# Row standard deviation: two adjacent rows per load, statistics split by columns between two engines, shrinking last pieces

## The chip, the cores and the metric

The kernel runs on one core of a Trainium2 chip. The time is the device time of one execution in microseconds (us), as the median of several executions. The profile is one such execution; its span leaves out about 1.8 us that the time includes (641.0 against 642.8 here). The experiments ran in four batches on four chips, and the kernel before took 642.6 us in the first comparison and about 645 us in these batches, so kernels are compared by their ratio to the kernel before on the same chip.

Five engines matter: DVE (VectorE), ACT (ScalarE), POOL (GpSimd), SP, which only issues loads and output writes here, and the 16 DMA engines, which carry all loads together.

## The reference

```python
x = np.random.randn(8192, 8192).astype(np.float32)
def reference(x):
    return np.std(x, axis=1)
```

268.4 MB are read once and 8192 numbers come out. Every row is held by one of 128 partitions; "a row" below means one row in each partition, 4 MiB in all.

## The kernel before

Partition p owns rows 64p to 64p+63, so in step i the kernel reads 128 runs of 32 KiB that lie 64 rows apart in the input. Five buffers of one row each are in turn. DVE sums a row, ACT sums its squares in two halves, and the variance follows from the two sums. The last row is loaded and summed in two halves.

```python
    xrows = x.rearrange("(p i) m -> i p m", p=P, i=I)      # I = 64, C = 8192, CS = 4096
    rows = [(i, [0, C]) for i in range(I - 1)] + [(I - 1, [0, CS, C])]    # shortened
    xpool = ctx.enter_context(tc.tile_pool(name="xtiles", bufs=5))
    # ... cut ...
    def do_row(i, cuts):
        xt = xpool.tile([P, C], FP32, name="xt")
        for ci in range(len(cuts) - 1):
            c0, c1 = cuts[ci], cuts[ci + 1]
            nc.sync.dma_start(out=xt[:, c0:c1], in_=xrows[i][:, c0:c1])
            nc.vector.reduce_sum(out=asum[:, i - base, ci:ci + 1], in_=xt[:, c0:c1], axis=mybir.AxisListType.X)
            # ... cut: nsub pieces of step columns ...
                nc.scalar.activation(out=dummy[:, 0:step], in_=xt[:, s0:s0 + step],
                    func=mybir.ActivationFunctionType.Square,
                    accum_out=asq[:, i - base, ci + si:ci + si + 1])
    # ... cut: the first 62 rows are combined on POOL, the last two on DVE, then Sqrt and two output writes
```

Of the kernel before, what the change touches and what calls it, by code (L numbers as in the profile page):

```python
# [1 line left out]

# [4 lines left out]

FP32 = mybir.dt.float32


@with_exitstack
def kernel(
    ctx: ExitStack,
    tc: tile.TileContext,
    x: bass.AP,
    out: bass.AP,
):
    nc = tc.nc
    P = nc.NUM_PARTITIONS  # L20
    R, C = x.shape
    I = R // P
    N = float(C)
    inv_n = 1.0 / N
    CS = C // 2

    xrows = x.rearrange("(p i) m -> i p m", p=P, i=I)
    out_pi = out.rearrange("(p i) -> p i", p=P)

    NB = I - 2  # L30
    rows = []
    for i in range(I - 1):
        rows.append((i, [0, C]))
    rows.append((I - 1, [0, CS, C]))

    xpool = ctx.enter_context(tc.tile_pool(name="xtiles", bufs=5))
    stats = ctx.enter_context(tc.tile_pool(name="stats", bufs=1))
    psum = ctx.enter_context(tc.tile_pool(name="psumdump", bufs=1, space=bass.MemoryType.PSUM))

    dummy = psum.tile([P, CS], FP32)  # L40

    NT = I - NB
    sumA = stats.tile([P, NB, 4], FP32)
    sqA = stats.tile([P, NB, 4], FP32)
    sumB = stats.tile([P, NT, 4], FP32)
    sqB = stats.tile([P, NT, 4], FP32)
    nc.vector.memset(sumB, 0.0)  # L47
    nc.vector.memset(sqB, 0.0)  # L48
    invn_t = stats.tile([P, 1], FP32)
    nc.vector.memset(invn_t, inv_n)  # L50

    def do_row(i, cuts):
        asum, asq, base = (sumA, sqA, 0) if i < NB else (sumB, sqB, NB)
        xt = xpool.tile([P, C], FP32, name="xt")
        for ci in range(len(cuts) - 1):
            c0, c1 = cuts[ci], cuts[ci + 1]
            nc.sync.dma_start(out=xt[:, c0:c1], in_=xrows[i][:, c0:c1])  # L57
            nc.vector.reduce_sum(  # L58
                out=asum[:, i - base, ci:ci + 1],
                in_=xt[:, c0:c1],  # L60
                axis=mybir.AxisListType.X,
            )
            nsub = (c1 - c0 + CS - 1) // CS
            step = (c1 - c0) // nsub
            for si in range(nsub):
                s0 = c0 + si * step
                nc.scalar.activation(  # L67
                    out=dummy[:, 0:step],
                    in_=xt[:, s0:s0 + step],
                    func=mybir.ActivationFunctionType.Square,  # L70
                    accum_out=asq[:, i - base, ci + si:ci + si + 1],
                )

    vA = stats.tile([P, NB], FP32)

    for (i, cuts) in rows:
        do_row(i, cuts)
        if i == NB - 1:
            tsqA = stats.tile([P, NB], FP32)
            nc.gpsimd.tensor_add(tsqA, sqA[:, :, 0], sqA[:, :, 1])  # L80
            t0 = stats.tile([P, NB], FP32)
            nc.gpsimd.tensor_mul(t0, sumA[:, :, 0], sumA[:, :, 0])  # L82
            nc.gpsimd.tensor_mul(t0, t0, invn_t.to_broadcast((P, NB)))  # L83
            nc.gpsimd.tensor_sub(vA, tsqA, t0)  # L84

    tsqB = stats.tile([P, NT], FP32)
    nc.vector.reduce_sum(out=tsqB, in_=sqB, axis=mybir.AxisListType.X)  # L87
    tsumB = stats.tile([P, NT], FP32)
    nc.vector.reduce_sum(out=tsumB, in_=sumB, axis=mybir.AxisListType.X)  # L89
    m2 = stats.tile([P, NT], FP32)  # L90
    nc.vector.scalar_tensor_tensor(  # L91
        out=m2, in0=tsumB, scalar=inv_n, in1=tsumB,
        op0=mybir.AluOpType.mult, op1=mybir.AluOpType.mult,
    )
    vB = stats.tile([P, NT], FP32)
    nc.vector.tensor_sub(vB, tsqB, m2)  # L96

    stdA = stats.tile([P, NB], FP32)
    nc.scalar.activation(out=stdA, in_=vA,  # L99
                         func=mybir.ActivationFunctionType.Sqrt, scale=inv_n)  # L100
    nc.sync.dma_start(out=out_pi[:, 0:NB], in_=stdA)
    stdB = stats.tile([P, NT], FP32)
    nc.scalar.activation(out=stdB, in_=vB,  # L103
                         func=mybir.ActivationFunctionType.Sqrt, scale=inv_n)
    nc.scalar.dma_start(out=out_pi[:, NB:I], in_=stdB)


# [1 line left out]
_INS = ['x']  # L109
_OUTS = [((8192,), 'float32')]  # L110


# [23 lines left out]
```

## Time and profile before

| what | value | where it stands |
|---|---|---|
| time | 642.79 us, 642.44 to 643.25 | three runs |
| DMA engines | 9 tenths or more in all but the first and last slices | page, busy tenths |
| a row lands every | 9.7 us, (39.8 + 8.7) / 5 | chain of waits |
| last input lands | 630.35 us | completion records |
| from there to the end | 10.7 us | 641.0 - 630.35 |

These are the last pieces of the chain of waits (start us, duration us, what):

```profile
571.74 8.70 DVE sumA L58
...
580.49 39.80 DMA xt<-in_x_dram
...
620.38 10.02 DVE sumB L58 x2
630.41 2.91 issue
633.31 4.41 DVE sumB L58
...
638.34 0.20 ACT stdB L103
```

Row 62 arrives at 620.3 us and row 63 at 630.35, but DVE needs 8.7 us a row and is busy until 637.7 (the 2.91 us that the chain calls issue are no idle time: DVE is at work on the first half of row 63). The stage table from 616 us on (stretch, length, busy time of DVE, ACT and POOL, clock, DMA share, GB/s) says the same:

```profile
616.00:620.00 4.00, 3.28 (x1) 3.39 (x3) 0.85 (x3) 1.00 0.90 385
620.00:624.00 4.00, 3.62 (x1) 3.54 (x2) 0.34 (x2) 1.00 1.00 426
624.00:628.00 4.00, 4.00 (x1) 3.97 (x4) 0.00 (x0) 1.00 0.97 410
628.00:632.00 4.00, 4.00 (x2) 3.94 (x4) 0.00 (x0) 1.00 0.14 51
632.00:636.00 4.00, 4.00 (x2) 3.54 (x2) 0.00 (x0) 1.00 0.00 0
636.00:640.00 4.00, 2.24 (x5) 0.20 (x1) 0.00 (x0) 1.00 0.02 0
```

### The profile page before, as it was taken

The numbers are of one execution on the slowest core, as the hardware profiler recorded it, in microseconds if no ns is written. First come the engines' busy times: TensorE is split into PE (matmuls) and PEld (weight loads), VectorE is DVE, ScalarE is ACT, GpSimd is POOL, SyncE is SP. The second block draws the span as 40 slices with busy tenths as digits, with TensorE's granted clock in tenths as the row PEclk, the third lists the DMA queues.
The fourth block names the chain that finished last, engine by engine and source line by source line (L and its number), as shares of the span: only waits on it lengthen the run. The fifth ranks groups of instructions, "written<-read, shape, count | busy, mean of one in ns | idle before, by whom it ended". The sixth has DMA issues, their size and how long they took to land.

```text
span 641.0 us, 576 instructions
## 1 busy us (share of the span) xinstructions
DVE 556.5 (87%) x72; ACT 477.9 (75%) x260; POOL 1.4 (0%) x8
## 2 busy tenths in 40 slices
DVE  1889889889889898898898898898898988988988
ACT  1767778778778778777787787787787787777886
POOL 0000000000000000000000000000000000000000
DMA  8999999999999999999999999999999999999992
GB/s 339 413 419 405 429 433 433 431 432 429 431 433 433 431 429 431 433 433 431 429 431 425 429 428 436 433 430 431 427 438 431 431 431 427 438 431 431 429 422 88
DMA packets 9653, 268.51 MB, mean 419 GB/s; under 512 B 1328, under 2 KB 1328, under 8 KB 1328
## 3 DMA queue, kind: packets, MB, share of 16 engines
q1 hardware_dynamic: 9504, 268.47, 97.9%
q14 instruction: 5, 0.04, 0.0%
q10 hardware_dynamic: 144, 0.00, 0.0%
HBM read 268.44 MB, written 0.03 MB: 419 GB/s over the span
## 4 chain that ended last, share of the span: by engine, by line
DMA 80%; DVE 19%; issue 1%; SPq 0%; ACT 0%; DVEq 0%
DMA xt<-in_x_dram 80%; DVE sumA L58 16%; DVE sumB L58 2%; SPq L57 0%; ACT stdB L103 0%; DVE vB L96 0%; DVE m L91 0%; DVE tsumB L89 0%; DVE tsqB L87 0%; DVEq L58 0%
## 5 line engine op out<-in xcount | busy, mean ns | idle before, releaser
L58 DVE TENSOR_REDUCE sumA<-xt 128x1 f32<-128x8192 f32 x62 | 538.5, 8686 | 79.8 <-DMA xt<-in_x_dram 79.8
L67 ACT ACTIVATE dummy<-xt 128x4096 f32<-128x4096 f32 x128 | 459.2, 3587 | 156.1 <-DMA xt<-in_x_dram 154.0
L67 ACT ACTIVATION_READ_ACCUMULATOR dummy<-xt 128x1 f32 x128 | 24.0, 187 | 0.0
L58 DVE TENSOR_REDUCE sumB<-xt 128x1 f32<-128x4096 f32 (+1 forms) x3 | 17.3, 5835 | 1.1 <-DMA xt<-in_x_dram 1.1
L103 ACT ACTIVATE stdB<-vB 128x2 f32<-128x2 f32 x1 | 0.2, 204 | 2.8 <-DVE vB L96 2.8
L67 ACT ACT_TABLE_LOAD x1 | 1.3, 1283 | 0.7 <-PEq L120 0.7
L80 POOL TENSOR_TENSOR tsqA<-sqA 128x62 f32<-128x62 f32 x1 | 0.3, 296 | 617.7 <-ACT dummy L67 617.7
L99 ACT ACT_TABLE_LOAD x1 | 1.3, 1283 | 0.0
L99 ACT ACTIVATE stdA<-vA 128x62 f32<-128x62 f32 x1 | 0.3, 257 | 1.0 <-POOL vA L84 1.0
L47 DVE MEMSET sumB<- 128x8 f32 x1 | 0.1, 65 | 0.8 <-PEq L120 0.8
L84 POOL TENSOR_TENSOR vA<-tsqA,t 128x62 f32<-128x62 f32 x1 | 0.3, 317 | 0.1
L82 POOL TENSOR_TENSOR t<-sumA 128x62 f32<-128x62 f32 x1 | 0.3, 295 | 0.9 <-DVE sumA L58 0.9
L83 POOL TENSOR_TENSOR t<-t,invn_t 128x62 f32<-128x62 f32 x1 | 0.3, 291 | 0.1
L96 DVE TENSOR_TENSOR vB<-tsqB,m 128x2 f32<-128x2 f32 x1 | 0.2, 161 | 0.0
L91 DVE SCALAR_TENSOR_TENSOR m<-tsumB 128x2 f32<-128x2 f32 x1 | 0.2, 160 | 0.0
L89 DVE TENSOR_REDUCE tsumB<-sumB 128x2 f32<-128x8 f32 x1 | 0.2, 161 | 0.0
L87 DVE TENSOR_REDUCE tsqB<-sqB 128x2 f32<-128x8 f32 x1 | 0.1, 149 | 0.0
L120 POOL MEMSET const-bfloat16-1.0<- 128x1 bf16 x1 | 0.1, 103 | 0.0
L120 POOL MEMSET const-uint8-127<- 128x1 uint8 x1 | 0.1, 103 | 0.0
L120 POOL MEMSET const-float32-0.0<- 128x1 f32 x1 | 0.1, 99 | 0.2 <-issue 0.2
L120 POOL MEMSET const-float32-1.0<- 128x1 f32 x1 | 0.1, 99 | 0.0
L48 DVE MEMSET sqB<- 128x8 f32 x1 | 0.1, 65 | 0.0
(1 smaller groups left out, 0.1 us busy)
## 6 DMA issues: line engine op xcount, KB each, us to landing
xt<-in_x_dram SPq DMA_DIRECT2D x63, 4096.0 KB, 39.8
xt<-in_x_dram SPq DMA_DIRECT2D x2, 2048.0 KB, 37.6
out_dram<-stdA SPq DMA_DIRECT2D x1, 31.0 KB, 9.8
out_dram<-stdB ACTq DMA_DIRECT2D x1, 1.0 KB, 1.4
```

What stands on the lines that cost most here:

```text
L58: nc.vector.reduce_sum(out=asum[:, i - base, ci:ci + 1], in_=xt[:, c0:c1], axis=mybir.AxisListType.X,)
L67: nc.scalar.activation(out=dummy[:, 0:step], in_=xt[:, s0:s0 + step], func=mybir.ActivationFunctionType.Square, accum_out=asq[:, i - base, ...
L80: nc.gpsimd.tensor_add(tsqA, sqA[:, :, 0], sqA[:, :, 1])
L82: nc.gpsimd.tensor_mul(t0, sumA[:, :, 0], sumA[:, :, 0])
L83: nc.gpsimd.tensor_mul(t0, t0, invn_t.to_broadcast((P, NB)))
L84: nc.gpsimd.tensor_sub(vA, tsqA, t0)
L89: nc.vector.reduce_sum(out=tsumB, in_=sumB, axis=mybir.AxisListType.X)
L91: nc.vector.scalar_tensor_tensor(out=m2, in0=tsumB, scalar=inv_n, in1=tsumB, op0=mybir.AluOpType.mult, op1=mybir.AluOpType.mult,)
L96: nc.vector.tensor_sub(vB, tsqB, m2)
L99: nc.scalar.activation(out=stdA, in_=vA, func=mybir.ActivationFunctionType.Sqrt, scale=inv_n)
L103: nc.scalar.activation(out=stdB, in_=vB, func=mybir.ActivationFunctionType.Sqrt, scale=inv_n)
L120: nc = _bacc.Bacc("TRN2", target_bir_lowering=False, num_devices=1)
```

## The change

The intent is a shorter end and fewer, larger loads. Each row is split by columns: DVE takes 5120 columns as ten statistics operations of 512 (mean and variance in one pass), ACT takes 3072 in two passes (squares and plain sum); of the last row ACT takes 1536. The pairs are combined by an aggregation on DVE and a few small POOL operations. Loads bring two rows of a partition, which lie next to each other in the input, as one run of 64 KiB; there are three buffers of two rows. The last row comes in pieces of 2048, 2048, 2048, 1024, 512, 256 and 256 columns, so that little is left to compute when the last one lands.

```diff
-    xpool = ctx.enter_context(tc.tile_pool(name="xtiles", bufs=5))
+    ACT_ROW = 3072
+    pieces = [(i, 0, C, ACT_ROW) for i in range(I - 2)]
+    pieces += [(I - 2, 0, C // 2, ACT_ROW // 2), (I - 2, C // 2, C // 2, ACT_ROW // 2)]
+    for n, a in ((2048, 512), (2048, 512), (2048, 512), (1024, 0), (512, 0), (256, 0), (256, 0)):
+        pieces.append((LAST, c0, n, a)); c0 += n          # joined here
+    bulk = ctx.enter_context(tc.tile_pool(name="bulk", bufs=3))
+    x2 = x.rearrange("(p i) m -> p (i m)", p=P, i=I)
+    def load(g):
+        xt = bulk.tile([P, 2 * C], FP32, name="xt")
+        base = 2 * g * C
+        if g < I // 2 - 2:
+            cuts = [(0, 2 * C)]
+        else:
+            cuts = [((r - 2 * g) * C + c0, n) for r, c0, n, _ in pieces if r // 2 == g]
+        for o, n in cuts:
+            nc.sync.dma_start(out=xt[:, o:o + n], in_=x2[:, base + o:base + o + n])
...
-            nc.vector.reduce_sum(... one row ...)
+        for d0 in range(a, n, F):                         # F = 512
+            nc.vector.bn_stats(out=bn[:, k * SD:(k + 1) * SD], in_=xt[:, d0:min(n, d0 + F)])
+            k += 1
+        if a:
+            nc.scalar.activation(out=dump[:, :a], in_=xt[:, :a], func=ACTF.Square, accum_out=q_act[:, r, j:j + 1])
+            nc.scalar.activation(out=dump[:, :a], in_=xt[:, :a], func=ACTF.Copy, accum_out=s_act[:, r, j:j + 1])
+        if c0 + n == C and r < LAST:
+            nc.vector.bn_aggr(out=agg[:, r, :], in_=bn)
... cut: eleven POOL operations combine the first 63 rows, seven the ACT part of the last row; Sqrt; output writes
```

More of the change, by code (lines that the diff above doesn't have):

```diff
@@ L9 @@
 FP32 = mybir.dt.float32
+ACTF = mybir.ActivationFunctionType
+ALU = mybir.AluOpType
 @with_exitstack
@@ L23 @@
     N = float(C)
-    inv_n = 1.0 / N
-    CS = C // 2
-    xrows = x.rearrange("(p i) m -> i p m", p=P, i=I)
+    F = nc.vector.BN_STATS_FMAX
+    SD = nc.vector.BN_STATS_DIM
+    LAST = I - 1
+    xr = x.rearrange("(p i) m -> p i m", p=P, i=I)
     out_pi = out.rearrange("(p i) -> p i", p=P)
-    NB = I - 2
-    rows = []
-    for i in range(I - 1):
-        rows.append((i, [0, C]))
-    rows.append((I - 1, [0, CS, C]))
-    xpool = ctx.enter_context(tc.tile_pool(name="xtiles", bufs=5))
+    ACT_ROW = 3072
@@ L37 @@
+    pieces = [(i, 0, C, ACT_ROW) for i in range(I - 2)]
+    pieces += [(I - 2, 0, C // 2, ACT_ROW // 2), (I - 2, C // 2, C // 2, ACT_ROW // 2)]
+    c0 = 0
+    for n, a in ((2048, 512), (2048, 512), (2048, 512), (1024, 0), (512, 0), (256, 0), (256, 0)):
+        pieces.append((LAST, c0, n, a))
+        c0 += n
+    N_D = float(C - ACT_ROW)
+    bulk = ctx.enter_context(tc.tile_pool(name="bulk", bufs=3))
     stats = ctx.enter_context(tc.tile_pool(name="stats", bufs=1))
+    bnp = ctx.enter_context(tc.tile_pool(name="bnp", bufs=3))
@@ L38 @@
     psum = ctx.enter_context(tc.tile_pool(name="psumdump", bufs=1, space=bass.MemoryType.PSUM))
-    dummy = psum.tile([P, CS], FP32)
-    NT = I - NB
-    sumA = stats.tile([P, NB, 4], FP32)
-    sqA = stats.tile([P, NB, 4], FP32)
-    sumB = stats.tile([P, NT, 4], FP32)
-    sqB = stats.tile([P, NT, 4], FP32)
-    nc.vector.memset(sumB, 0.0)
-    nc.vector.memset(sqB, 0.0)
-    invn_t = stats.tile([P, 1], FP32)
-    nc.vector.memset(invn_t, inv_n)
-    def do_row(i, cuts):
-        asum, asq, base = (sumA, sqA, 0) if i < NB else (sumB, sqB, NB)
-        xt = xpool.tile([P, C], FP32, name="xt")
-        for ci in range(len(cuts) - 1):
-            c0, c1 = cuts[ci], cuts[ci + 1]
-            nc.sync.dma_start(out=xt[:, c0:c1], in_=xrows[i][:, c0:c1])
-            nc.vector.reduce_sum(
-                out=asum[:, i - base, ci:ci + 1],
-                in_=xt[:, c0:c1],
-                axis=mybir.AxisListType.X,
-            )
-            nsub = (c1 - c0 + CS - 1) // CS
-            step = (c1 - c0) // nsub
-            for si in range(nsub):
-                s0 = c0 + si * step
-                nc.scalar.activation(
-                    out=dummy[:, 0:step],
-                    in_=xt[:, s0:s0 + step],
-                    func=mybir.ActivationFunctionType.Square,
-                    accum_out=asq[:, i - base, ci + si:ci + si + 1],
-                )
@@ L74 @@
-    vA = stats.tile([P, NB], FP32)
-    for (i, cuts) in rows:
-        do_row(i, cuts)
-        if i == NB - 1:
-            tsqA = stats.tile([P, NB], FP32)
-            nc.gpsimd.tensor_add(tsqA, sqA[:, :, 0], sqA[:, :, 1])
-            t0 = stats.tile([P, NB], FP32)
-            nc.gpsimd.tensor_mul(t0, sumA[:, :, 0], sumA[:, :, 0])
-            nc.gpsimd.tensor_mul(t0, t0, invn_t.to_broadcast((P, NB)))
-            nc.gpsimd.tensor_sub(vA, tsqA, t0)
-    tsqB = stats.tile([P, NT], FP32)
-    nc.vector.reduce_sum(out=tsqB, in_=sqB, axis=mybir.AxisListType.X)
@@ L88 @@
-    tsumB = stats.tile([P, NT], FP32)
-    nc.vector.reduce_sum(out=tsumB, in_=sumB, axis=mybir.AxisListType.X)
-    m2 = stats.tile([P, NT], FP32)
-    nc.vector.scalar_tensor_tensor(
-        out=m2, in0=tsumB, scalar=inv_n, in1=tsumB,
-        op0=mybir.AluOpType.mult, op1=mybir.AluOpType.mult,
-    )
-    vB = stats.tile([P, NT], FP32)
-    nc.vector.tensor_sub(vB, tsqB, m2)
-    stdA = stats.tile([P, NB], FP32)
-    nc.scalar.activation(out=stdA, in_=vA,
-                         func=mybir.ActivationFunctionType.Sqrt, scale=inv_n)
@@ L101 @@
-    nc.sync.dma_start(out=out_pi[:, 0:NB], in_=stdA)
-    stdB = stats.tile([P, NT], FP32)
-    nc.scalar.activation(out=stdB, in_=vB,
-                         func=mybir.ActivationFunctionType.Sqrt, scale=inv_n)
-    nc.scalar.dma_start(out=out_pi[:, NB:I], in_=stdB)
+    dump = psum.tile([P, ACT_ROW], FP32)
+    agg = stats.tile([P, I, 2], FP32)
+    s_act = stats.tile([P, I, 3], FP32)
+    q_act = stats.tile([P, I, 3], FP32)
+    nc.gpsimd.memset(s_act, 0.0)
+    nc.gpsimd.memset(q_act, 0.0)
@@ new lines @@
+    warm = stats.tile([P, 1], FP32)
+    nc.vector.memset(warm, 1.0)
+    nc.scalar.activation(out=warm, in_=warm, func=ACTF.Sqrt)
+    n_last = sum(-(-(n - a) // F) for r, _, n, a in pieces if r == LAST)
+    a_last = float(sum(a for r, _, n, a in pieces if r == LAST))
+    last_bn = stats.tile([P, 3 + n_last * SD], FP32)
+    x2 = x.rearrange("(p i) m -> p (i m)", p=P, i=I)
[8 more added lines that the diff above has]
+            nc.sync.dma_start(out=xt[:, o:o + n], in_=x2[:, base + o:base + o + n])
+        return xt
@@ new lines, with g @@
+    bn, k, j = None, 0, 0
+    for pi, (r, c0, n, a) in enumerate(pieces):
+        if r % 2 == 0 and c0 == 0:
+            pair = load(r // 2)
+        o = (r % 2) * C + c0
+        xt = pair[:, o:o + n]
+        if c0 == 0:
+            k, j = 0, 0
+            if r < LAST:
+                bn = bnp.tile([P, (C - ACT_ROW) // F * SD], FP32, name="bn")
+            else:
+                bn = last_bn[:, 3:]
+        for d0 in range(a, n, F):
+            d1 = min(n, d0 + F)
+            nc.vector.bn_stats(out=bn[:, k * SD:(k + 1) * SD], in_=xt[:, d0:d1])
+            k += 1
+        if a:
+            nc.scalar.activation(out=dump[:, :a], in_=xt[:, :a], func=ACTF.Square,
+                                 accum_out=q_act[:, r, j:j + 1])
+            nc.scalar.activation(out=dump[:, :a], in_=xt[:, :a], func=ACTF.Copy,
+                                 accum_out=s_act[:, r, j:j + 1])
+            j += 1
+        if c0 + n == C and r < LAST:
+            nc.vector.bn_aggr(out=agg[:, r, :], in_=bn)
+        if c0 + n == C and r == LAST - 1:
+            B = LAST
+            def g(nm):
+                return stats.tile([P, B], FP32, name=nm)
+            dm, dv = agg[:, 0:B, 0], agg[:, 0:B, 1]
+            ss, qq, t1, t2, t3, t4 = (g(f"g{z}") for z in range(6))
+            nd = stats.tile([P, 1], FP32)
+            nc.gpsimd.memset(nd, N_D)
+            ndb = nd.to_broadcast((P, B))
+            ninv = stats.tile([P, 1], FP32)
+            nc.gpsimd.memset(ninv, 1.0 / N)
+            ninvb = ninv.to_broadcast((P, B))
+            nc.gpsimd.tensor_add(ss, s_act[:, 0:B, 0], s_act[:, 0:B, 1])
+            nc.gpsimd.tensor_add(qq, q_act[:, 0:B, 0], q_act[:, 0:B, 1])
+            nc.gpsimd.tensor_mul(t1, dm, dm)
+            nc.gpsimd.tensor_add(t1, t1, dv)
+            nc.gpsimd.tensor_mul(t1, t1, ndb)
+            nc.gpsimd.tensor_add(t1, t1, qq)
+            nc.gpsimd.tensor_mul(t2, dm, ndb)
+            nc.gpsimd.tensor_add(t2, t2, ss)
+            nc.gpsimd.tensor_mul(t3, t2, t2)
+            nc.gpsimd.tensor_mul(t3, t3, ninvb)
+            nc.gpsimd.tensor_sub(t4, t1, t3)
+            std = stats.tile([P, B], FP32)
+            nc.scalar.activation(out=std, in_=t4, func=ACTF.Sqrt, scale=1.0 / N)
+            nc.sync.dma_start(out=out_pi[:, 0:B], in_=std)
+        if r == LAST and pi + 1 < len(pieces) and pieces[pi + 1][3] == 0 and a:
+            sl = stats.tile([P, 2], FP32)
+            an = stats.tile([P, 1], FP32)
+            nc.gpsimd.memset(an, 1.0 / a_last)
+            nc.gpsimd.memset(last_bn[:, 0:1], a_last)
+            nc.gpsimd.tensor_add(sl[:, 0:1], s_act[:, r, 0:1], s_act[:, r, 1:2])
+            nc.gpsimd.tensor_add(sl[:, 0:1], sl[:, 0:1], s_act[:, r, 2:3])
+            nc.gpsimd.tensor_add(sl[:, 1:2], q_act[:, r, 0:1], q_act[:, r, 1:2])
+            nc.gpsimd.tensor_add(sl[:, 1:2], sl[:, 1:2], q_act[:, r, 2:3])
+            nc.gpsimd.tensor_mul(last_bn[:, 1:2], sl[:, 0:1], an)
+            m2 = stats.tile([P, 1], FP32)
+            nc.gpsimd.tensor_mul(m2, last_bn[:, 1:2], sl[:, 0:1])
+            nc.gpsimd.tensor_sub(last_bn[:, 2:3], sl[:, 1:2], m2)
@@ L109 @@
+    nc.vector.bn_aggr(out=agg[:, LAST, :], in_=last_bn)
+    stdl = stats.tile([P, 1], FP32)
+    nc.scalar.activation(out=stdl, in_=agg[:, LAST, 1:2], func=ACTF.Sqrt)
+    nc.scalar.dma_start(out=out_pi[:, LAST:I], in_=stdl)
 _INS = ['x']
```

## The prediction

> **What bounds the kernel now.** The load stream. The page of the profile shows the DMA engines at 9 tenths or more in every slice but the first and the last, and 431 to 433 GB/s in most slices. The chain of waits is 80% "DMA xt" and repeats: 39.8 us for a load, 8.70 us for the DVE sum that frees its buffer. Five such steps overlap, so a row of 4 MiB lands every (39.8+8.7)/5 = 9.7 us, or 432 GB/s. DVE (8.69 us a row) and ACT (2 x 3.75 us) both idle each row, waiting for DMA. The Trainium skill, "DMA: Bandwidth & Descriptors", "Where 436 GB/s comes from", states a ceiling of 435.2 GB/s; the trace is within 1% of it.
>
> Row 62 lands at 620.3 us, so the last row should land near 630.0; the stage table shows DMA fading from 628 and silent from 630. The span ends at 641.0. So 11 us are exposed: DVE works until 637.7, then small operations, square root and output write.
>
> **What the change does.**
> - Bulk: same bytes, half as many loads. A row costs 9.715 us, against 9.64 us at the skill's 435.2 GB/s. If the difference of 0.08 us a row is per-descriptor or per-load cost, halving it gives an estimated 0 to 2.5 us over 64 rows. Most likely 1 us.
> - Compute: DVE gets 5120 columns as ten 512-column statistics operations. By the skill's "VectorE: DVE Perf Modes" (58 + FD cycles at 0.96 GHz), estimated at 0.6 us each, and 6.3 us a row with the aggregation. ACT makes two passes over 3072 columns; from 3.75 us per 4096-column pass here, 2.9 us each, 5.8 us a row. Both fall well below 9.7 us. DMA still sets the pace.
> - Buffers: three of two rows instead of five of one. A pair is consumed about 13 us after landing; the two loads behind it cover 38.8 us, so the queue stays fed.
> - Tail: the last pieces shrink to 256 columns. After the last landing remain one short statistics operation (0.4), aggregation (0.3), square root (0.2) and output write (2.4 us in before's end). But the instruction order puts the square root of the first 63 rows on ACT in front of the last row's second piece, and it waits for eleven dependent POOL operations at about 0.37 us. I estimate that ACT's last pieces are therefore done about 1 us after the last landing, followed by about 1.6 us of dependent POOL operations, and only then aggregation. Tail about 5.5 us, instead of 11.
>
> **Sum.** 641.0 - 5.5 (tail) - 1 (stream) = 634.5 us span; measured times stand 1.8 us above the span: 636. Range 631 to 641. Faster by over 2% (below 629.9): 8%; within 2%: 88%; slower by over 2%: 4%.
>
> **What would show it.** Landing of pairs every 19.3 to 19.45 us; GB/s 431 to 434 in the slices; DVE and ACT busy near 65% and 60%, idle before each pair ended by DMA; from last landing to end 4 to 7 us, with POOL-released idle on ACT and DVE there; 30 bulk loads of 8 MiB, time to landing near 45 us.
>
> **What would make it wrong.** The statistics operation needing two cycles an element: DVE would take 11 us a row and bound the kernel (slower by 10%). 64 KiB runs being slower, or landing unevenly over the 16 engines, so that three buffers leave some of them idle. A faster stream in the first 64 us, where before has 339 to 419 GB/s.

## More of the kernel before

The page of the kernel before. The lines give the span, the busy time of each engine, the DMA engines' share and rate in 40 equal slices, the instruction fetches, the shares of the chain of waits, and the two costliest groups with their idle time and what ended it:

```profile
span 641.0 us, 576 instructions
...
DVE 556.5 (87%) x72; ACT 477.9 (75%) x260; POOL 1.4 (0%) x8
...
DMA  8999999999999999999999999999999999999992
GB/s 339 413 419 405 429 433 433 431 432 429 431 433 433 431 429 431 433 433 431 429 431 425 429 428 436 433 430 431 427 438 431 431 431 427 438 431 431 429 422 88
...
q14 instruction: 5, 0.04, 0.0%
...
DMA xt<-in_x_dram 80%; DVE sumA L58 16%; DVE sumB L58 2%; SPq L57 0%; ACT stdB L103 0%; DVE vB L96 0%; DVE m L91 0%; DVE tsumB L89 0%; DVE tsqB L87 0%; DVEq L58 0%
...
L58 DVE TENSOR_REDUCE sumA<-xt 128x1 f32<-128x8192 f32 x62 | 538.5, 8686 | 79.8 <-DMA xt<-in_x_dram 79.8
L67 ACT ACTIVATE dummy<-xt 128x4096 f32<-128x4096 f32 x128 | 459.2, 3587 | 156.1 <-DMA xt<-in_x_dram 154.0
```

Both engines wait for data in every row, and the DMA engines never rest: the load stream sets the pace, with some loss in the first four slices.

## The result, and the profile after

The changed kernel takes 647.96 us (646.23 to 649.28, four runs) against 642.62 for the kernel before in the same rounds. The ratio is 1.0087, with a 95% interval of 1.0065 to 1.0109. A ratio is the mean time of one kernel's fast runs over that of the other's of the same rounds, so it is not quite the ratio of the medians. The change is within 2%, but on the other side of zero than forecast, and outside the range of 631 to 641.

The same lines of the page after:

```profile
span 646.1 us, 1166 instructions
...
DVE 407.7 (63%) x709; ACT 366.7 (57%) x272; POOL 5.1 (1%) x28
...
DMA  8999999999999999999999999999999999999993
GB/s 325 394 402 402 438 414 430 454 410 435 451 426 422 450 426 426 446 430 418 450 434 418 446 442 414 443 443 414 438 450 414 434 451 418 426 454 406 413 328 90
...
q14 instruction: 9, 0.07, 0.0%
...
DMA xt<-in_x_dram 79%; DVE bn L89 18%; DVE last_bn L89 1%; DVE agg L98 1%; SPq L72 0%; DVE agg L140 0%; ACT stdl L142 0%; DVEq L140 0%
...
L89 DVE BATCH_NORM_STATS2 bn<-xt 128x6 f32<-128x512 f32 x630 | 377.9, 675 | 229.8 <-DMA xt<-in_x_dram 229.8
L92 ACT ACTIVATE dump<-xt 128x3072 f32<-128x3072 f32 (+2 forms) x67 | 174.3, 2601 | 269.4 <-DMA xt<-in_x_dram 268.4
```

The engines behave as forecast, with DVE at 63% and ACT at 57% of the span and both waiting for DMA alone. The last slices of the rate line do not: 328 GB/s stands where before had 422. The stage table shows where:

```profile
616.00:620.00 4.00, 4.00 (x7) 3.97 (x3) 0.00 (x0) 1.00 0.95 408
620.00:624.00 4.00, 3.96 (x8) 3.65 (x6) 0.00 (x0) 1.00 1.06 299
624.00:628.00 4.00, 0.82 (x3) 0.65 (x1) 0.00 (x0) 1.00 0.97 242
628.00:632.00 4.00, 3.58 (x7) 3.22 (x6) 1.68 (x7) 1.00 0.98 237
632.00:636.00 4.00, 1.86 (x4) 1.70 (x5) 1.32 (x5) 1.00 0.75 199
636.00:640.00 4.00, 3.13 (x6) 2.17 (x7) 0.85 (x5) 1.00 0.14 50
```

Between 620 and 632 us the DMA engines are fully busy, yet they move 237 to 299 GB/s, 55 to 69% of the 431 of the steady stretch. They are not short of work; their packets take longer.

After the last input (640.5 us) the end is short. The timeline shows, first, ten statistics operations back to back for comparison, then DVE working off the last pieces and the aggregation following at once:

```profile
614.70 6.03 DVE L89 BATCH_NORM_STATS2 bn<-xt 128x6 f32<-128x512 f32 x10 [0.48 <-DMA xt<-in_x_dram]
...
637.97 4.31 DVE L89 BATCH_NORM_STATS2 last_bn<-xt 128x6 f32<-128x512 f32 x8 [0.87 <-DMA xt<-in_x_dram]
...
640.46 0.19 POOL L138 TENSOR_TENSOR last_bn<-sl,m 128x1 f32<-128x1 f32 x1
642.39 0.55 DVE L140 BATCH_NORM_AGGREGATE agg<-last_bn 128x2 f32<-128x87 f32 x1
642.97 0.20 ACT L142 ACTIVATE stdl<-agg 128x1 f32<-128x1 f32 x1 [3.46 <-DVE agg L140]
```

### Packets and landings

The trace also has every DMA packet with start, duration and size. Here each run of a partition is one packet, even the 64 KiB ones, and a DMA engine carries eight of a load's 128. A packet has a usual duration: 2418 ns for 64 KiB, 1213 for 32, 611 for 16, 309 for 8, 159 for 4, 84 for 2 and 46 for 1 KiB; in a run without slow packets (e4, below) the mean of each size is within 5% of that. "Slow" below is the time beyond the usual, summed over all packets and divided by the 16 engines. Each of a load's 16 engines reports its own completion, so that the landings show how far the engines are apart.

| us per DMA engine | before | after |
|---|---|---|
| usual time of all packets | 621.1 | 619.6 |
| slow, first 100 us | 3.8 | 6.5 |
| slow, 100 to 600 us | 2.1 | 1.1 |
| slow, from 600 us on | 0.1 | 6.0 |
| last input: mean of the 16 engines | 629.0 | 635.8 |
| last input: last engine | 630.35 | 640.52 |
| end of the span | 641.0 | 646.1 |

The end after the last input shrank by 5.1 us (10.7 to 5.6), and the last input came 10.2 us later. Of these 10.2, the mean engine is 6.8 us later: 7.6 more slow time, 1.5 less usual time, and 0.7 of gaps between packets and a later start (the first packets of the 16 engines start 0.5 us later on average). The remaining 3.4 are the distance of the last engine from the mean, which grew from 1.4 to 4.7 (both rounded). So there are two questions: what makes packets slow, and what separates the engines?

### The profile page after: what moved, and what is told of

Its sections match the earlier page's. It is cut to its first block, busy times and chain, and to the rows that moved or that the text cites. A ratio compares the mean times of both kernels' runs of the same rounds, so it can differ in the third digit from the quotient of the medians.

```text
span 646.1 us, 1166 instructions
## 1 busy us (share of the span) xinstructions
DVE 407.7 (63%) x709; ACT 366.7 (57%) x272; POOL 5.1 (1%) x28
## 4 chain that ended last, share of the span: by engine, by line
DMA 79%; DVE 20%; SPq 0%; issue 0%; ACT 0%; DVEq 0%
DMA xt<-in_x_dram 79%; DVE bn L89 18%; DVE last_bn L89 1%; DVE agg L98 1%; SPq L72 0%; DVE agg L140 0%; ACT stdl L142 0%; DVEq L140 0%
## 5 line engine op out<-in xcount | busy, mean ns | idle before, releaser
L89 DVE BATCH_NORM_STATS2 bn<-xt 128x6 f32<-128x512 f32 x630 | 377.9, 675 | 229.8 <-DMA xt<-in_x_dram 229.8
L92 ACT ACTIVATE dump<-xt 128x3072 f32<-128x3072 f32 (+2 forms) x67 | 174.3, 2601 | 269.4 <-DMA xt<-in_x_dram 268.4
L94 ACT ACTIVATE dump<-xt 128x3072 f32<-128x3072 f32 (+2 forms) x67 | 174.3, 2601 | 2.1
L98 DVE BATCH_NORM_AGGREGATE agg<-bn 128x2 f32<-128x60 f32 x63 | 26.3, 417 | 1.1
L92 ACT ACTIVATION_READ_ACCUMULATOR dump<-xt 128x1 f32 x67 | 12.5, 186 | 0.0
L94 ACT ACTIVATION_READ_ACCUMULATOR dump<-xt 128x1 f32 x67 | 12.5, 186 | 0.0
L89 DVE BATCH_NORM_STATS2 last_bn<-xt 128x6 f32<-128x512 f32 (+1 forms) x14 | 8.1, 642 | 3.4 <-DMA xt<-in_x_dram 3.4
```

The source lines that it names most:

```text
L89: nc.vector.bn_stats(out=bn[:, k * SD:(k + 1) * SD], in_=xt[:, d0:d1])
L92: nc.scalar.activation(out=dump[:, :a], in_=xt[:, :a], func=ACTF.Square, accum_out=q_act[:, r, j:j + 1])
L94: nc.scalar.activation(out=dump[:, :a], in_=xt[:, :a], func=ACTF.Copy, accum_out=s_act[:, r, j:j + 1])
L98: nc.vector.bn_aggr(out=agg[:, r, :], in_=bn)
```

## The experiments

Theory A: the short runs of the last row are slow. Theory B: the 64 KiB runs upset the stream. Theory C: what matters is that the 128 runs of a load lie 2 MiB apart. Theory F came later: fetching instructions sets single DMA engines back. Timed runs have five rounds. The packet figures of all runs stand together after the last of them.

### The last row in two halves (e1)

```diff
-            cuts = [... for r, c0, n, _ in pieces if r // 2 == g]
+            cuts = [... for r, c0, n, _ in pieces if r // 2 == g and r < LAST]
+            if g == I // 2 - 1:
+                cuts += [(C, C // 2), (C + C // 2, C // 2)]
```

> The changed kernel, with the last row loaded in two runs of 16 KiB per partition in place of seven shrinking ones; computing stays in the seven pieces. Theory A (the short last runs are what slows the stream at the end: 8 KiB packets took 474 ns on average instead of their usual 309, 4 KiB packets 312 instead of 159): packets at the end take their usual time, the stream ends some 5 us earlier, and although the last half row is then computed at once (about 3 to 4 us of DVE work exposed), the span is 2 to 5 us shorter than the changed kernel's 646. Theory B (the 64 KiB runs upset the whole stream and the end only shows it): the 16 KiB packets at the end are slow too (over 650 ns on average), and the span stays at 646 or longer.

Measured: 648.10 us, ratio 1.0054 (1.0031 to 1.0077). Slow time at the end fell from 6.0 to 1.3 us per engine, as theory A has it; but the 16 KiB packets of the last row averaged 685 ns (650 with those of row 62) in place of 611, which is over what theory B had named. The span did not move (645.9), against the 2 to 5 us expected: the start was slower than usual in the profiled run (9.7 us), so the last input came only 2.2 us earlier (638.3), and a half row was left to compute. (The 474 ns in the expectation counts instruction fetches of 8 KiB too; loads alone average 481.) Short runs are most of the slow end, but not all of it.

### Each pair as two loads (e2)

```diff
-            cuts = [(0, 2 * C)]
+            cuts = [(0, C), (C, C)]
```

> The changed kernel, with each pair of rows loaded by two transfers of 32 KiB runs into the same shared buffer. Theory A (short last runs): the end stays slow (8 KiB packets 450 to 500 ns); only the start improves. Start: the changed kernel loses 6.5 us per DMA engine to slow packets in the first 100 us, before loses 3.8; if the 64 KiB run is the cause, this run loses about 4; against that, 32 KiB packets need 1213 ns where half a 64 KiB packet needs 1209, worth 1.5 us over the stream. Net about 1 us shorter than the changed kernel, near 645. Theory B (64 KiB runs upset the whole stream): start and end both become as in before, and the span falls to 638 or less.

Measured: 648.79 us, ratio 1.0054 (1.0038 to 1.0071), span 649.0. The start lost 3.6 us, as before does, and the end still 5.9. So a 64 KiB run costs about 3 us at the start against a 32 KiB run (the five profiles that start with 64 KiB runs 2 MiB apart lost 6.5 to 9.7 us there, the three with 32 KiB runs 3.6 to 4.6), but it is not what makes the end slow: theory B falls. The expected gain did not come. In the profiled run the middle lost 5.1 us where the changed kernel loses 1.1; that run was the slowest of the six (650.78 us).

### The kernel before with small last loads (e3)

```diff
+            if i < I - 1:
                 nc.sync.dma_start(out=xt[:, c0:c1], in_=xrows[i][:, c0:c1])
+            elif ci == 0:
+                d0 = 0
+                for n in (2048, 2048, 2048, 1024, 512, 256, 256):
+                    nc.sync.dma_start(out=xt[:, d0:d0 + n], in_=xrows[i][:, d0:d0 + n])
+                    d0 += n
```

> The kernel before, with only its last row loaded in the seven shrinking pieces of the changed kernel; computing unchanged. Theory A (short last runs): its stream slows at the end, 8 KiB packets average over 400 ns, the last landing moves from about 630 to 635 us or later; DVE is busy with row 62 until 629 and then needs 8.7 us more, so the span grows by 0 to 4 us over 641. Theory B (64 KiB runs): 8 KiB packets take 309 ns, the last landing stays at 630 and the span at 641.

Measured: 649.65 us, ratio 1.0068 (1.0050 to 1.0086). The 8 KiB packets averaged 487 ns, slow time at the end was 5.6 us, and the last input landed at 639.4. The span was 647.1, more than the 0 to 4 us over 641 that were expected: DVE, which still takes the last half row in one sum, waited 2.96 us for it. Without any 64 KiB run, the small last loads alone make the end slow. Theory A is right about what the slow packets are; it does not say why.

### Runs 64 KiB apart in place of 2 MiB (e4)

```diff
-    x2 = x.rearrange("(p i) m -> p (i m)", p=P, i=I)
+    xg = x.rearrange("(g p t) m -> g p (t m)", p=P, t=2)
-            nc.sync.dma_start(out=xt[:, o:o + n], in_=x2[:, base + o:base + o + n])
+            nc.sync.dma_start(out=xt[:, o:o + n], in_=xg[g][:, o:o + n])
```

> The changed kernel, with neighbouring partitions reading neighbouring pairs of rows, so that the 128 runs of one transfer lie 64 KiB apart in the input in place of 2 MiB; the results come out in the wrong order on purpose. Theory C (packets are slow where the engines read at the same place of rows that lie 2 MiB apart, at the start while they are in step and at the end where short runs hold them to the same place): slow packets at the start (6.5 us per engine) and at the end (6.0 us per engine) both fall below 2 us each, and the span falls to 636 or less. If the spacing has no part in it, the span stays at 646 with the same slow packets.

Measured: 636.16 us, ratio 0.9858 (0.9845 to 0.9872), span 634.0. The loads are as large and the last pieces as short as in the changed kernel; only the distance in the input differs. Slow time fell to 0.7 us at the start and 0.3 at the end, and the 8 KiB packets averaged 315 ns. Theory C holds as far as the distance goes; that the engines read at the same place of their rows at the same time, as the expectation has it, is not shown. The results stand in the wrong order on purpose. The comparison with the reference did not notice: all 8192 results are near 1, so this check cannot see a wrong order, and where results below are called rightly ordered, that rests on the row assignment in the code.

### The same at 1984 KiB (e7), and the changed kernel again (e8)

Is it nearness that helps, or getting away from the power of two? Here a partition owns 62 rows of the first 7936, and two of the last 256.

```diff
-    x2 = x.rearrange("(p i) m -> p (i m)", p=P, i=I)
+    xb = x[0:NB * P].rearrange("(p i) m -> p (i m)", p=P, i=NB)      # NB = 62
+    xe = x[NB * P:R].rearrange("(p i) m -> p (i m)", p=P, i=2)
-            nc.sync.dma_start(out=xt[:, o:o + n], in_=x2[:, base + o:base + o + n])
+            src = xb[:, base + o:base + o + n] if 2 * g < NB else xe[:, o:o + n]
+            nc.sync.dma_start(out=xt[:, o:o + n], in_=src)
... and the output writes to match
```

> The changed kernel with another assignment of rows: partition p reads rows 62p to 62p+61, so that the 128 runs of one transfer lie 1984 KiB apart in place of 2048, and the last 256 rows go two to a partition, 64 KiB apart. Results in the right order. If the exact power of two is the cause of the slow packets, they vanish at the start and the end as they did with 64 KiB spacing (below 2 us per engine in each), and the span is 633 to 636. If it was nearness that helped, the start keeps its 6 us and the span is 639 or more.

> The changed kernel again, unedited, on the chip on which the next three run, so that they can be set against it: 0.5 to 0.9% slower than before. Slow packets again about 6 us per DMA engine in the first 100 us and 6 us at the end, and one DMA engine lands its share of the last pieces some 3 us after the other fifteen.

Measured on one chip: the changed kernel 650.77 us, ratio 1.0098 (1.0060 to 1.0137); with 62 rows 637.41 us, ratio 0.9881 (0.9862 to 0.9901). The changed kernel is again slower than before, by 1.0%, just over what was expected; its end lost 6.3 us, and its last engine came 1.9 us after the fifteenth, not 3. Its six executions scatter from 648.0 to 655.6 us (the profile is of the fastest), the five with 62 rows from 637.2 to 637.8. The start's slow time is 6.9 us in the first and 0.7 in the second. These are the first 60 us of each in the stage table, the changed kernel first (the profile of the comparison; e8's has 6.9 us of slow time there, it has 6.5):

```profile
0.00:20.00 20.00, 0.06 (x1) 1.49 (x2) 0.80 (x10) 1.00 0.93 351
20.00:40.00 20.00, 12.67 (x22) 11.43 (x8) 0.00 (x0) 1.00 0.99 383
40.00:60.00 20.00, 12.49 (x22) 11.42 (x8) 0.00 (x0) 1.00 1.01 413
```

```profile
0.00:20.00 20.00, 0.06 (x1) 1.49 (x2) 0.79 (x10) 1.00 1.00 419
20.00:40.00 20.00, 12.66 (x22) 11.43 (x8) 0.00 (x0) 1.00 0.97 419
40.00:60.00 20.00, 12.66 (x22) 11.43 (x8) 0.00 (x0) 1.00 0.97 420
```

The last column rises from 351, 383 and 413 GB/s to 419 or 420. A distance 3% shorter than 2 MiB is as good as one of 64 KiB at the start. Of the three distances tried, 2048 KiB alone costs; other powers of two were not tried. The end of this run says nothing on that, since its last rows lie 64 KiB apart. The end of e11, below, does: there the last pair lies 1984 KiB apart, and its 8 KiB packets average 313 ns, with 0.2 us of slow time.

### Only the last pair 64 KiB apart (e12)

```diff
+    xn = x[0:2 * P].rearrange("(p t) m -> p (t m)", p=P, t=2)
-            nc.sync.dma_start(out=xt[:, o:o + n], in_=x2[:, base + o:base + o + n])
+            src = x2[:, base + o:base + o + n] if g < I // 2 - 1 else xn[:, o:o + n]
+            nc.sync.dma_start(out=xt[:, o:o + n], in_=src)
```

> The changed kernel, with only the last pair of rows read 64 KiB apart (it reads the first 256 rows of the input over again, so the last two results of each partition are wrong on purpose); the other 31 pairs stay 2 MiB apart. It takes the end apart from the start. If short runs slow down only where they are 2 MiB apart, the 8 KiB packets take 309 to 320 ns and the slow packets of the end fall from 6 us per DMA engine to below 1, while the start keeps its 6; the last landing comes at 632 to 635 in place of 640.5 and the span is 638 to 641. If the end is slow because the engines are out of step, the span stays at 646.

Measured: 644.36 us, ratio 0.9991 (0.9959 to 1.0023), span 641.8. The end's slow time fell to 0.5 us, with 8 KiB packets at 311 ns, while the start kept 7.9. So start and end are slow independently of each other, and being out of step does not make the end slow: the engines were 7 us apart here too. The last input landed at 636.2, a little later than expected, and the span is 0.8 us over the range; the start, which lost 7.9 us in place of 6, would account for both. The stage table of its end, where the changed kernel had 242 and 237 GB/s at a DMA share near 1:

```profile
624.00:628.00 4.00, 3.61 (x7) 3.12 (x5) 0.30 (x1) 1.00 1.01 422
628.00:632.00 4.00, 3.36 (x7) 2.55 (x8) 2.71 (x10) 1.00 0.77 303
```

### The kernel before at 1984 KiB (e5), and with idle copies (e6)

In the run at 64 KiB spacing, where slow packets are gone, one engine still lagged. Its last input reached 15 of the 16 engines by 623.8 us and the last one at 628.4. The distance between the first and the last engine grew in steps of about 1 us, each just after an instruction fetch of 8 KiB on queue 14:

```
e4: us of a landing : us between its first and last engine
61:1.0  139:1.0  178:1.9  256:1.9  295:2.9  373:2.9  413:3.8  490:3.9  530:4.8  612:4.8  620:5.8
fetches that go before a step:   170.2    287.3    397.1    514.2    617.3
```

Packets do not name their engine, but where one ends and the next starts can be matched. At the first four of these fetches the engine concerned has a gap of 0.31 us between two packets, and the packet after the gap takes 0.66 us longer than usual. Other fetches leave smaller steps: 0.5 us after the one at 58.1 us, and 0.7 on another engine after the one at 419.0. The changed kernel has 709 DVE instructions where before has 72. Theory F: more instructions, more fetches, one engine later. The test adds eight copies of one element in each of the first 62 rows to the kernel before, both at 1984 KiB so that slow packets do not hide it.

```diff
             nc.vector.reduce_sum(... one row ...)
+            for z in range(8 if i < NB else 0):
+                nc.vector.tensor_copy(out=tiny[:, z:z + 1], in_=xt[:, c0:c0 + 1])
```

> The kernel before with the same assignment of rows (1984 KiB apart), nothing else. Slow packets of the first 100 us fall from 3.8 us per DMA engine to below 1, the last landing moves from 630.5 to about 626 us, the span from 641 to about 637. With only one DVE instruction a row few instructions are fetched, so under theory F (an instruction fetch sets back the one DMA engine that carries it by 1 us, and the last landing waits for that engine) the sixteen engines stay within 1.5 us of each other up to the end.

> The run above plus eight one-element DVE copies in each of the first 62 rows, which DVE has time for (8.69 + about 0.6 us of 9.7): some 500 more instructions, none of them on the path of the end. Theory F: four more instruction fetches in the stream, each sets one DMA engine back by about 1 us, the spread of the landings grows in steps to 4 us or more, and the last landing and the span come 3 to 4 us later than without the copies. If fetches cost only their own 0.33 us, or are shared by all engines, the span is within 1 us of the run above.

Measured on one chip: 640.18 us without the copies, ratio 0.9923 (0.9904 to 0.9943), and 642.76 us with them, ratio 0.9963 (0.9945 to 0.9981). The page, without and with:

```profile
DVE 556.5 (87%) x72; ACT 477.7 (75%) x260; POOL 1.4 (0%) x8
...
q14 instruction: 5, 0.04, 0.0%
```

```profile
DVE 586.5 (92%) x568; ACT 477.7 (75%) x260; POOL 1.4 (0%) x8
...
q14 instruction: 8, 0.07, 0.0%
```

Three more fetches; the spread of the landings rises in three steps of 1 us (at about 200, 340 and 480 us) and one of 0.7, to 4.2 in place of 2.4; the last input comes 1.8 us later, and the time is 2.6 us longer. The time grows by more than the last input's delay because DVE, once row 62 is in, works without a pause to the end, and row 62 came 2.4 us later. These are the last sums, without and with the copies:

```profile
616.44 17.34 DVE L61 TENSOR_REDUCE sumB<-xt 128x1 f32<-128x8192 f32 x3 [1.12 <-DMA xt<-in_x_dram]
```

```profile
618.88 17.34 DVE L63 TENSOR_REDUCE sumB<-xt 128x1 f32<-128x8192 f32 x3 [0.56 <-DMA xt<-in_x_dram]
```

The copies themselves cost nothing on the way, since DVE still waits for data (0.54 us before the sum of row 61). Nor do they slow the stream by holding buffers longer: the mean of the 16 engines has the last input only 0.2 us later (625.0 against 624.8). It is the last engine that falls behind. The expected 3 to 4 us were too many, because the run without copies is not free of fetches either: its spread reaches 2.4 us where I had written 1.5. The Trainium skill, "Perfetto Trace Analysis", "The 4-stage abstract model", states that instructions have 64 bytes, so an 8 KiB fetch holds 128. With nine DVE instructions a row that is a fetch every 14 rows, an estimated 137 us; the run has DVE's fetches at 55.8, 192.8, 339.5 and 476.5 us, 137 to 147 us apart.

### The changed kernel with few instructions (e10)

```diff
+        if r < WHOLE:                                     # WHOLE = I - 6 = 58
+            nc.vector.reduce_sum(out=s_act[:, r, 0:1], in_=xt, axis=mybir.AxisListType.X)
+            for h in range(2):
+                nc.scalar.activation(out=dump, in_=xt[:, h * C // 2:(h + 1) * C // 2],
+                                     func=ACTF.Square, accum_out=q_act[:, r, h:h + 1])
+            continue
```

> The changed kernel with few instructions: the first 58 rows are summed as in before (one DVE sum of 8192 columns, two ACT squares), the statistics operations stay for the last six rows alone; loads, row assignment (2 MiB apart) and end unchanged. Theory F (instruction fetches set one DMA engine back, seen by itself in the pair of runs with and without tiny copies): no steps of 1 us in the spread of the landings, no single engine that lands its last share some 3 us after the other fifteen, last landing at about 637.5 in place of 640.5 and the span about 643 in place of 646. The slow packets of start and end stay, about 6 us per engine each. If the span stays at 646, the fetches were hidden behind the slow packets.

Measured: 648.01 us, ratio 1.0061 (1.0020 to 1.0102), span 645.7. The single straggler is gone (the last input reached the last three engines at 639.4, 639.5 and 640.1), but the last of them is hardly earlier than in the changed kernel (640.5), and the intervals of the two ratios overlap. The span stayed, as the expectation's last sentence had allowed. That does not show that fetches cost nothing at 2 MiB. In the profiled run the start lost 8.1 us in place of 6.5, and the mean of the 16 engines had the last input at 637.2 in place of 635.8; the distance from the mean to the last engine shrank from 4.7 to 2.9 us. And the changed kernel's own trace has the steps: the distance between its first and last engine grows by 1.0 us after each of three fetches (294.2, 404.1 and 521.2 us), with the same gap and the same slow packet as in e4, and its last engine came 3.0 us after the fifteenth. How much of the 5 us of the change is due to fetches, this run leaves open. Slow packets separate the engines too: with few instructions the last engine was still 2.9 us behind the mean here and 1.9 in e3.

Taken over all profiles, the last engine is 4.3 to 5.9 us behind the mean in the seven with statistics operations in every row, at either spacing, and 1.0 to 2.9 us in the six with few instructions (e6, with the copies, has 3.6).

### Both causes taken away (e9), and its end mended (e11)

e9 joins the edits of e7 and e10, with one more:

```diff
-    for n, a in ((2048, 512), (2048, 512), (2048, 512), (1024, 0), (512, 0), (256, 0), (256, 0)):
+    for n, a in ((2048, 1024), (2048, 1024), (2048, 1024), (1024, 0), (512, 0), (256, 0), (256, 0)):
```

> The same few instructions, with the rows 1984 KiB apart and, for the last row, ACT taking 1024 columns of each 2048 in place of 512. Meant as a version that beats both kernels, results in the right order. Both causes taken away: the 64 KiB runs need 619.6 us of an engine, slow packets take about 2 more, the last landing should be at about 625, the end after it 5 us, the span 630 and the time 632, against 637.4 with the row assignment alone and 640.2 for before with it. If fetches cost nothing here, the span stays at 635.

Measured: 634.50 us, ratio 0.9827 (0.9804 to 0.9851), span 632.7: better than both kernels, with the last input at 624.2 as forecast, and the engines within 1.6 us of each other. But the end took 8.5 us in place of 5. The timeline:

```profile
627.36 0.19 POOL L151 TENSOR_TENSOR last_bn<-sl,m 128x1 f32<-128x1 f32 x1
627.58 0.47 DVE L153 BATCH_NORM_AGGREGATE agg<-last_bn 128x2 f32<-128x69 f32 x1 [2.15 <-POOL last_bn L151]
```

Here the aggregation does wait for POOL. ACT now had more of the last row, and the square root of the first 63 rows, which stands among its squares, had waited for POOL until 620.38. Besides, the last output write took 2.84 us from issue to landing against 1.47 in the changed kernel; it writes 4 bytes every 8 bytes.

```diff
-            src = xb[:, base + o:base + o + n] if 2 * g < NB else xe[:, o:o + n]
+            src = xe[:, o:o + n] if g == 0 else xb[:, base - 2 * C + o:base - 2 * C + o + n]
... the Sqrt of the first 63 rows and its writes moved behind the POOL operations of the last row; the last result goes to another address
```

> The best version so far (few instructions, rows 1984 KiB apart; span 632.7) with two defects of its end mended: the square root of the first 63 rows no longer stands in front of the last row's squares on ACT, where it waited for POOL and delayed the last aggregation by 2.15 us, and the last output write goes to addresses 248 bytes apart in place of 8 (it took 2.8 us from its issue to landing, 1.5 in the changed kernel). Results in the right order. Expected: last input landing at 624.2 as before, DVE done at 625.5, aggregation at once, span 629.5, time 631 to 632. If the write's landing does not depend on the spacing, 632.5.

Measured: 633.04 us, ratio 0.9803 (0.9778 to 0.9828), span 631.0. The write landed in 1.44 us, so its spacing of 8 bytes was the cost. (e5, e6 and e7 write their last results as closely and took 2.8 to 3.2 us, the runs with the old output layout 1.4 to 1.5; so their gains from the row assignment are some 1.5 us larger than their times show.) The other mend had no effect: the compiled order put the square root back in its old place (it runs at 620.09), and the aggregation again waits 2.11 us for POOL. Those 2 us are still to be had; how they would be had was not tried.

### All packet figures together

| run | slow, first 100 us | slow, from 600 us | 8 KiB packet, mean ns | last input | engines apart | span | ratio |
|---|---|---|---|---|---|---|---|
| before | 3.8 | 0.1 | - | 630.4 | 2.6 | 641.0 | 1 |
| after | 6.5 | 6.0 | 481 | 640.5 | 8.9 | 646.1 | 1.0087 |
| e1 halves | 9.7 | 1.3 | - | 638.3 | 7.4 | 645.9 | 1.0054 |
| e2 two loads a pair | 3.6 | 5.9 | 496 | 644.1 | 8.5 | 649.0 | 1.0054 |
| e3 before, small last loads | 4.6 | 5.6 | 487 | 639.4 | 4.6 | 647.1 | 1.0068 |
| e4 after, 64 KiB apart | 0.7 | 0.3 | 315 | 628.4 | 5.7 | 634.0 | 0.9858 |
| e12 after, last pair 64 KiB apart | 7.9 | 0.5 | 311 | 636.2 | 7.1 | 641.8 | 0.9991 |
| e7 after, 1984 KiB apart | 0.7 | 0.3 | 315 | 628.4 | 6.0 | 635.9 | 0.9881 |
| e5 before, 1984 KiB apart | 0.8 | 0.1 | - | 626.8 | 2.4 | 638.6 | 0.9923 |
| e6 the same with copies | 0.7 | 0.1 | - | 628.6 | 4.2 | 640.9 | 0.9963 |
| e10 after, few instructions | 8.1 | 6.2 | 502 | 640.1 | 5.5 | 645.7 | 1.0061 |
| e9 both | 0.7 | 0.2 | 314 | 624.2 | 1.6 | 632.7 | 0.9827 |
| e11 both, end mended | 0.7 | 0.2 | 313 | 623.9 | 1.2 | 631.0 | 0.9803 |

Packet figures and spans are of the one profiled run, ratios of all timed ones.

## Why the prediction was wrong, point by point

- **What bounds the kernel: right.** The load stream set the pace before and after. The usual packet time gives 16 x 65536 B / 2418 ns = 433.7 GB/s, within 0.4% of the 435.2 that the Trainium skill, "DMA: Bandwidth & Descriptors", "Where 436 GB/s comes from", states.
- **"Bulk: ... estimated 0 to 2.5 us over 64 rows. Most likely 1 us": this step failed.** Its own subject was sized well: the usual time of all packets fell by 1.5 us per engine. What it left out was everything beyond the usual. It took the 9.7 us a row of the steady stretch for the pace of all rows, the first and the last included. The start lost 2.7 us more than before, and the end lost 6.0, of which 5.4 on packets of 8 and 4 KiB, 2 MiB apart; the last engine then came 3.4 us further behind the mean. In place of 1 us earlier, the last input came 10.2 us later.
- **What was at hand.** The profile of the kernel before already showed the start at 339 to 419 GB/s, and the prediction named it only as a chance to be faster. The page cited above was at hand too: its section "Latency and other measured facts" has a row that copies between tensors of a 2 MiB row pitch run below full rate. The prediction does not use it. e4, e7 and e12 show that the pitch counts where the runs are short and where the stream begins.
- **Compute: right.** Ten statistics operations take 6.03 us in the timeline, 0.60 each in a row of them. The Trainium skill, "VectorE: DVE Perf Modes", in its section on the trn2 errata, has 58 + FD cycles, 0.594 us for 512; the pace in the trace agrees, though a single one is recorded at 675 ns, overlapping the next.
- **Buffers: right as far as it shows.** Between 100 and 600 us the stream lost 1.1 us of slow time, less than before.
- **Tail "about 5.5 us, instead of 11": right in size (5.6 against 10.7), wrong in the chain, so the match in size is luck.** I had POOL releasing the aggregation. POOL was done at 640.65; DVE's own statistics ended at 642.28, since eight of them were left when the third large piece landed. The POOL chain came true only in e9 and e11, where ACT had more to do.
- **"Landing unevenly over the 16 engines" stood among what could go wrong, with little weight.** It took 3.4 us of the 10.2, though not by idling engines for want of buffers: the last landing simply waits for the slowest engine. Both slow packets and the instruction fetches of the many statistics operations separate the engines; how the 3.4 us divide between them is not shown.

Had the rows been 1984 KiB apart in both kernels, e7 and e5, run on one chip, say what the change is worth: 637.41 against 640.18 us, 2.8 us less. With its many instructions taken away and another share of the last row (e9), more: a ratio of 0.9827 against 0.9923 for e5, on another chip.

What stays open: why packets are slow at exactly 2 MiB. That the same memory channels are hit together is a natural reading, and the skill's row gives it as an inference too; no run here shows it. Why the long runs of the steady stretch are spared although they also lie 2 MiB apart is open as well, and so is the mild slowness of the 16 KiB halves in e1 (685 ns for 611).

## What to carry to other kernels

Here the steady load rate said nothing about the first and the last loads. Before cutting the last pieces small, look at how far apart the runs of one load lie in memory; here moving from 2 MiB to 1984 KiB (the last two rows to 64 KiB) was worth more (0.8% for the kernel before, 2.2% for the changed one, by the ratios on one chip) than the whole rewrite. Where the work waits for the last load, as in the changed kernel, the slowest of the 16 DMA engines sets the end, so compare their landings, and count instructions: about every 128 of them is a fetch that one of these engines has to carry.

## What the Trainium skill lacked or had wrong

- "DMA: Bandwidth & Descriptors", "Latency and other measured facts", gives 164 GB/s for copies of 16 KiB runs between HBM tensors at a 2 MiB row pitch (with 214 as full rate), without telling steady stretches from starts or longer from shorter runs, and calls for padding by a few KiB. Loads into SBUF at this pitch, in runs of 32 and 64 KiB, ran at 431 and 432 GB/s once under way (100 to 600 us, before and after). They were slow in the first 100 us (351, 383, 413 GB/s in its first three fifths) and in short runs (8 KiB packets 481 to 502 ns on average, usually 309; 4 KiB 289 to 312, usually 159). Giving each partition 62 rows in place of 64 was enough.
- "SBUF — State Buffer" and "DMA: Bandwidth & Descriptors" advise large loads in their rules for kernel authors, and say nothing of small last ones: pieces down to 128 KiB in all lost 0.3 us per engine to slow packets at 64 KiB spacing (e4), 0.2 at 1984 KiB (e11) and about 6 at 2 MiB.
- No page says that an instruction fetch sets back the DMA engine that carries it, here by 0.5 to 1 us under full load (0.31 us for itself and up to 0.66 us in the packet after it), or that the last landing waits for that engine. The DMA page, "Queues, rings and completion order", names row 14 as internal to the runtime, with refills in its list; the runs show it as queue 14 with one 8 KiB packet for about every 128 instructions of an engine.
- No page gives the cost of the statistics operations: 0.60 us for 512 columns in a row of them (675 ns recorded for one), 0.55 us for the last aggregation.
- No page says that the spacing of tiny output writes matters: 128 writes of 4 bytes landed 2.84 us after their issue at 8 byte spacing (e9), and 1.44 us at 248 bytes (e11).
